# Moving operands of each layer at a byte offset of their own, and a weight ring of four slots, in a four-block encoder

## The chip, the cores and the metric

The kernel runs on one core of a Trainium2 chip. The metric is the device time of one execution in microseconds (us), taken as the median of several runs. The engines are named as in the profile: PE is the matrix engine, PEld its loading of weights, DVE the vector engine, ACT the scalar engine, POOL the general one, and SP issues the DMA transfers.

## What is computed

The reference is a four-block encoder on a sequence of 256 tokens with 1024 features, in float32. Each block has a gated feed-forward layer, a mixer and a second feed-forward layer, so there are twelve layers:

```python
for i in range(DEPTH):                       # DEPTH = 4
    m, j = i % 3, i // 3
    x = x + 0.5 * swiglu(rms_norm(x, norms[i, 0]), ffn_w_in[i, 0], ffn_w_out[i, 0])
    hn = rms_norm(x, norms[i, 1])
    y = short_conv_mixer / hyena_mixer / gated_deltanet_mixer   # m = 0 / 1 / 2
    x = x + y
    x = x + 0.5 * swiglu(rms_norm(x, norms[i, 2]), ffn_w_in[i, 1], ffn_w_out[i, 1])
return rms_norm(x, final_norm)
```

The feed-forward width is 2816, which is 22 tiles of 128. The layers in order are: feed-forward, short convolution, feed-forward, feed-forward, Hyena, feed-forward, feed-forward, gated delta rule, feed-forward, feed-forward, short convolution, feed-forward. The code numbers them by `ng`, 0 to 11.

## The kernel before

Everything that is multiplied by a weight goes through one helper, `mm3`. A float32 number is split into a high part of type fp32r and the remainder, also fp32r, and a product is three matmuls of 128 x 128 weights against 128 x 256 moving columns: high weights with high columns (L324), low weights with high columns (L325), high weights with low columns (L326). The weights are the stationary operand and the tokens the moving one.

**Weights.** All weights are packed on the host into 665 parts of 128 x 1024. `load_group` brings them in two at a time (1 MB, two buffers of two parts). `cut_part` splits a part: ACT writes the high part `wh` (L279), then DVE the low part `wl` (L281). Both go into a ring of RING = 5 slots for each of `wh` and `wl`. One part is used by 24 matmuls. A slot is free again when the last of its 24 matmuls is done.

**Moving operands.** At the end of a layer `split_x` writes the residual stream times the next norm's weight as `xh` (ACT, L344) and `xl` (DVE, L345), four pairs of tiles of 128 x 512, which the next layer's projections read (the tiles `g`, `c`, `b`, `p`, `x`, `xv` in PSUM). Inside a layer `split` writes the activations as `hh` (ACT, L454) and `hl` (DVE, L455), 128 x 256, four slots each, which the output products read (`accf`, `accs`, `acch`, `accd`). A feed-forward layer has 44 projection parts and 22 output parts.

**Layer starts.** `finish` holds the last two parts of a layer at the same time and goes through the four PSUM banks of the output product bank by bank: as soon as a bank is complete, DVE updates `x` (L438, in the Hyena layer L432), and `split_x` and `square_x` follow. The next layer begins with `proj_first`, which takes three parts side by side, so that the last tiles of `x` are wanted late: 6 matmuls of each of the three parts for a first pair of tiles, then again for the second, and so on. The fourth and fifth parts of a layer are held back until the last split of `x` has been issued (`behind`).

**Order of the work.** The program is written in the order of the mathematics; a scheduler of the framework orders the instructions of each engine by its own estimate of when their inputs and buffers are free. Each engine then runs its list strictly in order.

**Places in memory.** From the program's memory map, in bytes within a partition: the ten ring slots begin at 47,360 + 4,096 n, and every 128-column block of weights 512 bytes on, so all weights of the ring begin 256 bytes above a multiple of 512. The tiles `xh` and `xl` also begin 256 above a multiple of 512, `hh` and `hl` 320 above one. For the rest of the text the *distance* of a matmul is the start of its moving operand less the start of its weights, modulo 512. In the kernel before it is 0 for all projections and 64 for the output products. In the Hyena layer the transforms `vf` and `vi`, whose operands are other tiles, have 256, and the last four output parts, whose `hh` and `hl` lie in another pool, have 320.

Of the kernel before, what the change touches and what calls it, by code (L numbers as in the profile page):

```python
# [11 lines left out]
F32 = mybir.dt.float32  # L12
F32R = mybir.dt.float32r
# [5 lines left out]
P = 128  # L19
D = 1024  # L20
L = 256
# [11 lines left out]
RING = 5  # L33
HOLD = 2
VACT = 3
WARM = 16

# [13 lines left out]
# ---------------------------------------------------------------- layouts  # L51
# Weight parts [128, 1024]: ("c", W, c0) = columns c0..c0+127 of W, all 8
# contraction tiles side by side; ("r", W, r0) = rows r0..r0+127 of W.
def out_tiles(f, n):
    """Rows of the output product that follow the projection of tile f."""
    if f <= LAG:
        return []
    lo = 0 if f == LAG + 1 else f - LAG
    return [t for t in range(lo, f - LAG + 1) if t < n - TAIL]
# [120 lines left out]
def shape_tables():  # L180
    f = np.float32
    # masks and ones
# [3 lines left out]
    # positional features of the filter network, transposed  # L186
# [11 lines left out]
    # 512-point transform of 256 samples, frequencies 0..255 and, in place of  # L198
    # the zero sine, the Nyquist one
# [15 lines left out]
# ---------------------------------------------------------------- program  # L215
class Prog:
    def __init__(self, nc, tc, io, phases, pools):
        self.nc, self.tc, self.io, self.phases = nc, tc, io, phases
        self.cp, self.rp, self.tp, self.ps = pools
        self.nparts = len(part_list(phases))  # L220
        self.next_part = 0
        self.raw = {}
# [3 lines left out]
        n = 0  # L226
# [9 lines left out]
    # ---- weight stream  # L236
    def load_group(self, lo, n):
        nc = self.nc
        t = self.rp.tile([P, GRP, D], F32, name=f"raw{lo}", tag="raw", bufs=RAW)
        if lo < 5:  # L240
            # the first parts come in small pieces
# [9 lines left out]
    def load_behind(self, dst, src):  # L251
        """A load that keeps its place behind the weights."""
        with self.tc.issue_after(self.load.ins):
            self.load = self.nc.sync.dma_start(dst, src)
# [31 lines left out]
    def behind(self, i, z):  # L286
        """Parts that a new phase wants late are split behind the split of x."""
# [10 lines left out]
    # ---- products: out[col, tok] (+)= part' @ x  # L298
# [10 lines left out]
    def proj_first(self, outs):  # L309
        """A phase's first products: several parts side by side, so that the  # L310
        last tiles of x are wanted late. outs: (destination, start)."""
# [19 lines left out]
    # ---- residual update, split of x*g, and 1/rms  # L331
# [4 lines left out]
    def split_x(self, m, ng):  # L336
        nc = self.nc
        ph = self.tp.tile([P, 512], F32R, name=f"xh{ng}_{m}", tag=f"xh{m}", bufs=1)
        pl = self.tp.tile([P, 512], F32R, name=f"xl{ng}_{m}", tag=f"xl{m}", bufs=1)
        for k in (2 * m, 2 * m + 1):  # L340
            s = slice((k % 2) * L, (k % 2 + 1) * L)
            xs, xh, xl = self.x[m][:, s], ph[:, s], pl[:, s]
# [18 lines left out]
    def rstd(self, ng, squared=False):  # L361
        """1/rms of the tokens, on every partition. Two stages, each to be
        issued behind other products."""
# [28 lines left out]
    # ---- accumulation of the output product  # L392
# [16 lines left out]
    def finish(self, pend, scale, bias, nxt):  # L409
        """The last output products, bank by bank, each bank's part of the  # L410
        residual stream updated as soon as it is complete."""
# [37 lines left out]
    def split(self, src, name, pool=None):  # L449
        """High and low parts of an SBUF tile."""  # L450
        pool = pool or self.tp
        hh = pool.tile([P, L], F32R, name=f"hh{name}", tag="hh", bufs=4)
        hl = pool.tile([P, L], F32R, name=f"hl{name}", tag="hl", bufs=4)
# [7 lines left out]
    # ---- phases  # L461
# [37 lines left out]
    def conv3(self, out, u, w, j, on_act=True):  # L499
        """out[t] = w0 u[t-1] + w1 u[t] + w2 u[t+1] along the free axis."""  # L500
# [50 lines left out]
    # ---- hyena: filters (spectra of the two-sided filter), then the mixer  # L551
    def sine(self, out, pre, bias, freq, tag):
        """out = sin(freq * (pre + bias)), the argument brought into [-pi, pi]."""
# [16 lines left out]
    def hy_setup(self):  # L570
        """Filter network up to its last layer; the rest goes to the background."""
# [42 lines left out]
        for c in range(2):  # L614
# [3 lines left out]
            def taps(b, c=c, cs=cs, eo=eo):  # L618
# [8 lines left out]
                if b == 0:  # L627
                    nc.vector.memset(hs[1][0:1, :], 0.0)
                    # v * d_bias is the filter's tap at zero
# [34 lines left out]
    def hy(self, ng, nxt):  # L664
# [6 lines left out]
        # constants of the short convolution: b_in enters through its taps  # L671
# [13 lines left out]
        def conv(pt, j, tag, bufs):  # L685
            """short convolution of one bank: columns j[0], j[1] of 128 features"""
# [28 lines left out]
        def turn(pr):  # L715
            """the pair's gated values with tokens on partitions"""
# [98 lines left out]
    # ---- gated delta rule, chunks of 128 tokens, both directions. With A the  # L815
    # strictly triangular matrix of a chunk, columns scaled by
    # gamma = beta / |k|^2, the chunk's solution is w = gamma * (I + A)^-1 r and
    # all products use the unscaled k and q.
    def gd(self, ng, nxt):
# [33 lines left out]
        # a large negative exponent outside the triangles  # L853
# [17 lines left out]
        def gates2(ab):  # L871
# [8 lines left out]
            # log(1 + exp(x)) = max(x, 0) + 2 atanh(u / (2 + u)), u = exp(-|x|)  # L880
# [28 lines left out]
        def decay(rg, hg, b, d):  # L909
            """E[s, c] = exp(sum of g over the tokens after s up to c), 0 outside the triangle"""  # L910
# [8 lines left out]
        def weights():  # L919
            """exp of the sums of g from a token to its chunk's end or start"""  # L920
# [17 lines left out]
        def turn(srcs, name):  # L938
            """[features, tokens] of two heads -> one bank [tokens, block, head, features]"""
# [45 lines left out]
        def kk(pr):  # L985
            """B = transposed -A of both directions"""
# [5 lines left out]
        def later():  # L992
            """Pool's work that nothing waits for yet"""
# [28 lines left out]
        # -- inverses of the 32 x 32 diagonal blocks, one block per partition  # L1022
        inv = {}

        def gather():
# [16 lines left out]
            # M[c, s] and the inverse's transpose X[s, c]; the two 16 x 16 blocks of the diagonal  # L1042
# [11 lines left out]
        def corner(stage, q):  # L1054
            """lower left 16 x 16 block: the second block's inverse times M21 times the first's"""
# [517 lines left out]
```

## Time and profile before

| quantity | value |
|---|---|
| median of 3 runs | 2073.7 us (2072.6 to 2074.67) |
| span of the profiled execution | 2073.3 us |
| PE busy | 2048.9 us, 99% |
| PEld busy | 2028.2 us, 98% |
| DVE busy | 1407.5 us, 68% |
| ACT busy | 1014.2 us, 49% |
| DMA | 356.76 MB, mean 172 GB/s |

The profile counts a matmul from its start to its modelled end, and successive matmuls overlap in it. A matmul that is listed with 283 ns therefore does not take 283 ns of the engine. What one costs is the distance between two starts, which the timeline shows, and which the text calls the pace. The program has few places at which PE stands idle, so that the span is close to the number of matmuls times their pace.

### The profile page before, as it was taken

To read this page: it belongs to the slowest core of one execution; us is meant where nothing else is said; L and a number is where in the kernel's file an instruction comes from. 1 tells how busy PE (TensorE), PEld (TensorE's weight loads), DVE (VectorE), ACT (ScalarE), POOL (GpSimd) and SP (SyncE) were. 2 spreads that over 40 slices of the span, in tenths; PEclk is the share of its full clock that TensorE was granted. 3 is DMA by queue.
4 is the path that set the end of the run, shared out by engine and by line. 5 is a ranking of instruction groups with operands and counts; after the bars stand their busy time and mean duration, and the time that the engine had idled before them with its cause. 6 is when DMAs were issued, how large, how long until landed. Compare 5 with 4: busy or idle time off the path is not lost.

```text
span 2073.3 us, 40294 instructions
## 1 busy us (share of the span) xinstructions
PE 2048.9 (99%) x17234; PEld 2028.2 (98%) x17234; DVE 1407.5 (68%) x2155; ACT 1014.2 (49%) x1546; POOL 73.8 (4%) x75
## 2 busy tenths in 40 slices
PE   9999999999999999999999998999999999999998
PEld 9999999999999999999999998899999999999998
DVE  6766867666666798666766689866667666767664
ACT  6444545445444555444544476555445444545443
POOL 0000000000000110000000021000000000000000
PEclk9999999999999999999999999999999999999999
DMA  7644455555555443555555532315554555555552
GB/s 249 233 164 153 153 183 183 183 183 173 194 183 184 163 158 128 196 184 187 181 184 185 185 123 102 123 62 185 184 184 169 199 185 185 179 185 181 186 186 95
DMA packets 93990, 356.76 MB, mean 172 GB/s; under 512 B 5810, under 2 KB 7218, under 8 KB 93619
## 3 DMA queue, kind: packets, MB, share of 16 engines
q1 hardware_dynamic: 93666, 354.18, 50.1%
q8 instruction: 135, 2.21, 0.4%
q14 instruction: 45, 0.36, 0.1%
q10 hardware_dynamic: 144, 0.00, 0.0%
HBM read 353.11 MB, written 1.05 MB: 171 GB/s over the span
## 4 chain that ended last, share of the span: by engine, by line
PE 89%; DVE 7%; DMA 2%; ACT 1%; issue 1%; POOL 0%; SPq 0%; POOLq 0%; DVEq 0%; ACTq 0%
PE g L324 16%; PE g L326 16%; PE g L325 16%; PE accf L324 8%; PE accf L326 8%; PE accf L325 8%; DVE wl L281 2%; PE c L324 1%; PE c L326 1%; PE c L325 1%; DMA raw<-w 1%; PE b L325 1%; PE b L324 1%; PE b L326 1%; PE accs L324 1%
## 5 line engine op out<-in xcount | busy, mean ns | idle before, releaser
L281 DVE TENSOR_TENSOR wl<-raw,wh 128x1024 fp32r<-128x1024 f32 (+1 forms) x667 | 811.2, 1221 | 430.7 <-ACT wh L279 430.3
L279 ACT ACTIVATE wh<-raw 128x1024 fp32r<-128x1024 f32 (+1 forms) x667 | 696.1, 1051 | 670.4 <-PE g L326 476.5
L324 PE MATMUL g<-xh,wh 128*128 128x256 f32 x2816 | 799.6, 284 | 1.0 <-ACT xh L344 0.7
L326 PE MATMUL g<-xl,wh 128*128 128x256 f32 x2816 | 798.3, 283 | 0.0
L325 PE MATMUL g<-xh,wl 128*128 128x256 f32 x2816 | 797.4, 283 | 0.3 <-DVE wl L281 0.3
L324 PEld LDWEIGHTS g<-xh,wh 128*128 128x128 f32 x2816 | 540.5, 192 | 4.1 <-ACT wh L279 2.8
L325 PEld LDWEIGHTS g<-xh,wl 128*128 128x128 f32 x2816 | 539.9, 192 | 0.6 <-DVE wl L281 0.5
L326 PEld LDWEIGHTS g<-xl,wh 128*128 128x128 f32 x2816 | 539.9, 192 | 0.2 <-DVE xl L345 0.2
L324 PE MATMUL accf<-hh,wh 128*128 128x256 f32 x1408 | 394.8, 280 | 0.0
L326 PE MATMUL accf<-hl,wh 128*128 128x256 f32 x1408 | 393.0, 279 | 0.0
L325 PE MATMUL accf<-hh,wl 128*128 128x256 f32 x1408 | 392.9, 279 | 0.0
L324 PEld LDWEIGHTS accf<-hh,wh 128*128 128x128 f32 x1408 | 264.9, 188 | 1.2 <-ACT hh L454 0.8
L326 PEld LDWEIGHTS accf<-hl,wh 128*128 128x128 f32 x1408 | 264.5, 188 | 0.0
L325 PEld LDWEIGHTS accf<-hh,wl 128*128 128x128 f32 x1408 | 264.2, 188 | 0.1
L454 ACT ACTIVATE hh<-t 128x256 fp32r<-128x256 f32 x192 | 79.8, 416 | 194.0 <-DVE t L474 189.7
L471 DVE TENSOR_TENSOR t<-g,rs 128x256 f32<-128x256 f32 x176 | 74.5, 423 | 83.8 <-PE g L326 77.2
L455 DVE TENSOR_TENSOR hl<-t,hh 128x256 fp32r<-128x256 f32 x192 | 81.4, 424 | 69.8 <-ACT hh L454 69.8
L325 PE MATMUL p<-xh,wl 128*128 128x256 f32 x256 | 74.5, 291 | 8.1 <-DVE wl L281 8.1
L472 ACT ACTIVATE t<-t 128x256 f32<-128x256 f32 x176 | 71.0, 404 | 23.4 <-DVE t L471 23.2
L324 PE MATMUL p<-xh,wh 128*128 128x256 f32 x256 | 75.8, 296 | 1.4 <-ACT wh L279 1.4
L474 DVE TENSOR_TENSOR t<-t,t 128x256 f32<-128x256 f32 x176 | 73.5, 418 | 1.5 <-ACT t L472 1.4
L326 PE MATMUL p<-xl,wh 128*128 128x256 f32 x256 | 74.1, 290 | 0.0
(315 smaller groups left out, 2424.7 us busy)
## 6 DMA issues: line engine op xcount, KB each, us to landing
raw<-w SPq DMA_DIRECT2D x330, 1024.0 KB, 4.8
raw<-w SPq DMA_DIRECT2D x6, 256.0 KB, 5.4
x<-x SPq DMA_DIRECT2D x4, 256.0 KB, 4.8
raw<-w SPq DMA_DIRECT2D x2, 512.0 KB, 6.1
dec<-dec SPq DMA_DIRECT2D x1, 1024.0 KB, 7.0
traw<-dft SPq DMA_DIRECT2D x2, 512.0 KB, 6.2
out<-ob SPq DMA_DIRECT2D x4, 256.0 KB, 2.4
w<-w SPq DMA_DIRECT2D x1, 512.0 KB, 9.0
```

Of the source, the lines that this page charges most:

```text
L279: nc.scalar.activation(hi[:, s], src[:, s], AF.Copy)
L281: nc.vector.tensor_tensor(lo[:, s], src[:, s], hi[:, s].bitcast(F32), op=ALU.subtract)
L324: mm(out, ah, bh, start=start, stop=False, skip_group_check=True)
L325: mm(out, al, bh, start=False, stop=False, skip_group_check=True)
L326: mm(out, ah, bl, start=False, stop=stop, skip_group_check=True)
L454: self.nc.scalar.activation(hh, src, AF.Copy)
L455: self.nc.vector.tensor_tensor(hl, src, hh.bitcast(F32), op=ALU.subtract)
L471: nc.vector.tensor_tensor(t1, pg[f][:, :L], self.rs, op=ALU.mult)
L472: nc.scalar.activation(t1, t1, AF.Silu)
L474: nc.vector.tensor_tensor(t2, t1, t2, op=ALU.mult)
```

## The change

Three things are changed. First, `xh`, `xl`, `hh` and `hl` move into a pool of their own, `mv`, that lies right behind the weights' ring and begins with 256 bytes that nothing uses (`lead`); their slots are 512 bytes longer than the tile (640 columns instead of 512, and 384 instead of 256). Second, the tile begins in its slot at FIRST[ng] columns, a different number in each of the twelve layers. Third, the ring has four slots instead of five, which gives back 8 KB of the 8.25 KB that this needs. In the gated delta rule `xtile` follows its slots into the new pool.

```diff
-RING = 5
+RING = 4
+LEAD = 64
+FIRST = (0, 8, 16, 32, 24, 48, 64, 40, 80, 96, 56, 112, 0)
...
+        self.mv.tile([P, LEAD], F32, name="lead")
...
     def split_x(self, m, ng):
-        ph = self.tp.tile([P, 512], F32R, name=f"xh{ng}_{m}", tag=f"xh{m}", bufs=1)
-        pl = self.tp.tile([P, 512], F32R, name=f"xl{ng}_{m}", tag=f"xl{m}", bufs=1)
+        ph = self.mv.tile([P, 640], F32R, name=f"xh{ng}_{m}", tag=f"xh{m}", bufs=1)
+        pl = self.mv.tile([P, 640], F32R, name=f"xl{ng}_{m}", tag=f"xl{m}", bufs=1)
         for k in (2 * m, 2 * m + 1):
             s = slice((k % 2) * L, (k % 2 + 1) * L)
-            xs, xh, xl = self.x[m][:, s], ph[:, s], pl[:, s]
+            at = slice((k % 2) * L + FIRST[ng], (k % 2 + 1) * L + FIRST[ng])
+            xs, xh, xl = self.x[m][:, s], ph[:, at], pl[:, at]
...
     def split(self, src, name, pool=None):
-        pool = pool or self.tp
-        hh = pool.tile([P, L], F32R, name=f"hh{name}", tag="hh", bufs=4)
-        hl = pool.tile([P, L], F32R, name=f"hl{name}", tag="hl", bufs=4)
+        pool = pool or self.mv
+        at = FIRST[int(name.split("_")[0])]
+        hh = pool.tile([P, 384], F32R, name=f"hh{name}", tag="hh", bufs=4)[:, at:at + L]
+        hl = pool.tile([P, 384], F32R, name=f"hl{name}", tag="hl", bufs=4)[:, at:at + L]
...
         def xtile(tag, name):
-            return self.tp.tile([P, 4, P], F32, name=name, tag=tag, bufs=1)
+            pool = self.tp if tag.startswith("sq") else self.mv
+            return pool.tile([P, 4, P], F32, name=name, tag=tag, bufs=1)
```

In the memory map of the changed program the ring still begins at 47,360, so the weights stay 256 bytes above a multiple of 512, and the slots of `xh`, `xl`, `hh` and `hl` begin at multiples of 512. Projections and output products of one layer now have the same distance, four times FIRST less 256, modulo 512:

| layer `ng` | 0 | 1 | 2 | 3 | 4 | 5 | 6 | 7 | 8 | 9 | 10 | 11 |
|---|---|---|---|---|---|---|---|---|---|---|---|---|
| kind | ff | conv | ff | ff | Hyena | ff | ff | delta | ff | ff | conv | ff |
| offset, bytes | 0 | 32 | 64 | 128 | 96 | 192 | 256 | 160 | 320 | 384 | 224 | 448 |
| distance before, projections | 0 | 0 | 0 | 0 | 0 | 0 | 0 | 0 | 0 | 0 | 0 | 0 |
| distance now | 256 | 288 | 320 | 384 | 352 | 448 | 0 | 416 | 64 | 128 | 480 | 192 |

The number of instructions of each kind stays, and so does the order of SP and POOL. What moves is the place of the weights' splits among the rest on ACT and DVE, since the scheduler has one slot less.

At the start of layer 3 (part 164 is its first, `wh166` and `wl166` belong to the third part of `proj_first`) ACT had this row before:

```order
L454 ACTIVATE hh2_21_5779<-t2_2_21_5774 128x256
L279 ACTIVATE wh166_5923<-raw165_5917 128x1024
L344 ACTIVATE xh3_0_5842<-x0_69,par_67 128x256 x2
L352 ACTIVATE sq3_0_5848<-x0_69 128x512
L344 ACTIVATE xh3_1_5863<-x1_70,par_67 128x256 x2
L352 ACTIVATE sq3_1_5869<-x1_70 128x512
L344 ACTIVATE xh3_2_5885<-x2_71,par_67 128x256 x2
```

Now ACT has this one:

```order
L460 ACTIVATE hh2_21_5783<-t2_2_21_5778 128x256
L283 ACTIVATE wh165_5923<-raw165_5921 128x1024
L349 ACTIVATE xh3_0_5846<-x0_73,par_71 128x256 x2
L357 ACTIVATE sq3_0_5852<-x0_73 128x512
L283 ACTIVATE wh166_5927<-raw165_5921 128x1024
L349 ACTIVATE xh3_1_5867<-x1_74,par_71 128x256 x2
L357 ACTIVATE sq3_1_5873<-x1_74 128x512
L349 ACTIVATE xh3_2_5889<-x2_75,par_71 128x256 x2
```

The third part's high split moved from ahead of the splits of `x` into their middle. On DVE, at the same place, before:

```order
L281 TENSOR_TENSOR wl166_5924<-raw165_5917,wh166_5923 128x1024
L438 SCALAR_TENSOR_TENSOR x0_69<-accf2_0_3987,x0_69 128x512
L345 SCALAR_TENSOR_TENSOR xl3_0_5843<-x0_69,par_67,xh3_0_5842 128x256
L438 SCALAR_TENSOR_TENSOR x1_70<-accf2_1_3988,x1_70 128x512
L345 SCALAR_TENSOR_TENSOR xl3_0_5843<-x0_69,par_67,xh3_0_5842 128x256
L438 SCALAR_TENSOR_TENSOR x2_71<-accf2_2_3989,x2_71 128x512
L345 SCALAR_TENSOR_TENSOR xl3_1_5864<-x1_70,par_67,xh3_1_5863 128x256 x2
L438 SCALAR_TENSOR_TENSOR x3_72<-accf2_3_3990,x3_72 128x512
```

And now:

```order
L285 TENSOR_TENSOR wl165_5924<-raw165_5921,wh165_5923 128x1024
L443 SCALAR_TENSOR_TENSOR x0_73<-accf2_0_3991,x0_73 128x512
L350 SCALAR_TENSOR_TENSOR xl3_0_5847<-x0_73,par_71,xh3_0_5846 128x256
L443 SCALAR_TENSOR_TENSOR x1_74<-accf2_1_3992,x1_74 128x512
L350 SCALAR_TENSOR_TENSOR xl3_0_5847<-x0_73,par_71,xh3_0_5846 128x256
L443 SCALAR_TENSOR_TENSOR x2_75<-accf2_2_3993,x2_75 128x512
L285 TENSOR_TENSOR wl166_5928<-raw165_5921,wh166_5927 128x1024
L350 SCALAR_TENSOR_TENSOR xl3_1_5868<-x1_74,par_71,xh3_1_5867 128x256 x2
L350 SCALAR_TENSOR_TENSOR xl3_2_5890<-x2_75,par_71,xh3_2_5889 128x256 x2
L443 SCALAR_TENSOR_TENSOR x3_76<-accf2_3_3994,x3_76 128x512
```

The third part's low split now stands behind the third update of `x`. It stands so at nine of the eleven layer starts. At the start of layer 5, behind the Hyena layer, DVE now has the third part's split (`wl264`) almost at the end of the splits of `x`, where before it stood ahead of them all:

```order
L437 SCALAR_TENSOR_TENSOR x3_76<-acch4_3_9236,par_71,x3_76 128x256
L350 SCALAR_TENSOR_TENSOR xl5_2_9613<-x2_75,par_71,xh5_2_9612 128x256 x2
L437 SCALAR_TENSOR_TENSOR x3_76<-acch4_3_9236,par_71,x3_76 128x256
L350 SCALAR_TENSOR_TENSOR xl5_3_9627<-x3_76,par_71,xh5_3_9626 128x256
L285 TENSOR_TENSOR wl264_9654<-raw263_9647,wh264_9653 128x1024
L350 SCALAR_TENSOR_TENSOR xl5_3_9627<-x3_76,par_71,xh5_3_9626 128x256
```

The start of layer 1 has the third part's split (`wl68`) in the same way just ahead of the last pair `xl1_3`.

## Rows read from the trace of the kernel before

**Rows 1.** The page, first part, and the chain that ended last.

```profile
PE 2048.9 (99%) x17234; PEld 2028.2 (98%) x17234; DVE 1407.5 (68%) x2155; ACT 1014.2 (49%) x1546; POOL 73.8 (4%) x75
...
PE 89%; DVE 7%; DMA 2%; ACT 1%; issue 1%; POOL 0%; SPq 0%; POOLq 0%; DVEq 0%; ACTq 0%
```

**Rows 2.** Stretch of two feed-forward layers: busy us (count) by engine, clock, DMA.

```profile
core 0: us, PE busy (x) PEld busy (x) DVE busy (x) ACT busy (x) POOL busy (x), PEclk, DMA share, GB/s
840.00:1180.00 340.00, 340.00 (x2852) 340.00 (x2852) 211.37 (x292) 155.24 (x210) 3.01 (x2) 1.00 0.55 185
```

**Rows 3.** The page's groups: busy, mean ns of one | idle before, releaser.

```profile
L281 DVE TENSOR_TENSOR wl<-raw,wh 128x1024 fp32r<-128x1024 f32 (+1 forms) x667 | 811.2, 1221 | 430.7 <-ACT wh L279 430.3
L279 ACT ACTIVATE wh<-raw 128x1024 fp32r<-128x1024 f32 (+1 forms) x667 | 696.1, 1051 | 670.4 <-PE g L326 476.5
```

**Rows 4.** Timeline of PE, start us and us: first and last of four rows.

```profile
539.43 0.28 PE L324 MATMUL accf<-hh,wh 128*128 128x256 f32 x1
...
542.15 0.28 PE L326 MATMUL accf<-hl,wh 128*128 128x256 f32 x1
542.26 0.29 PE L324 MATMUL g<-xh,wh 128*128 128x256 f32 x1
...
547.91 0.28 PE L326 MATMUL g<-xl,wh 128*128 128x256 f32 x1
...
786.22 0.28 PE L324 MATMUL acch<-hh,wh 128*128 128x256 f32 x1
...
788.92 0.28 PE L326 MATMUL acch<-hl,wh 128*128 128x256 f32 x1
...
791.91 0.28 PE L324 MATMUL acch<-hh,wh 128*128 128x256 f32 x1
...
799.96 0.28 PE L326 MATMUL acch<-hl,wh 128*128 128x256 f32 x1
```

**Rows 5.** Tiles `vf` and `sp`: ns min/median/max, first and last start us.

```profile
L325 PE MATMUL vf<-vth,tl x32: 278/283/283, 724.0 to 791.7; 128*128 128x256 f32 x32
...
L325 PE MATMUL sp<-eoh,tl x4: 389/389/389, 250.5 to 252.5; 128*128 128x512 f32 x4
...
L325 PE MATMUL sp<-eoh,tl x2: 393/395/397, 157.1 to 157.8; 128*128 128x512 f32 x2
```

**Rows 6.** Timeline at the start of layer 3: ACT, DVE, PE.

```profile
499.11 1.04 ACT L279 ACTIVATE wh<-raw 128x1024 fp32r<-128x1024 f32 x1
...
502.86 0.62 ACT L352 ACTIVATE sq<-x 128x512 f32<-128x512 f32 x1
...
503.99 0.68 DVE L438 SCALAR_TENSOR_TENSOR x<-accf,x 128x512 f32<-128x512 f32 x1
...
509.87 2.35 DVE L281 TENSOR_TENSOR wl<-raw,wh 128x1024 fp32r<-128x1024 f32 x2
...
504.33 0.29 PE L324 MATMUL g<-xh,wh 128*128 128x256 f32 x1
...
513.34 0.36 PE L324 MATMUL g<-xh,wh 128*128 128x256 f32 x1
```

**Rows 7.** Timeline at the start of layer 5: DVE, PE.

```profile
815.01 0.47 DVE L345 SCALAR_TENSOR_TENSOR xl<-x,par,xh 128x256 fp32r<-128x256 f32 x1
...
812.55 0.28 PE L324 MATMUL g<-xh,wh 128*128 128x256 f32 x1
```

**Rows 8.** Tile `wl` from 1200 to 1330 us, delta-rule layer: who waited for it.

```profile
  PEld p L325: 8.5, 2
```

More of the change, by code (lines that the diff above doesn't have):

```diff
@@ L218, in __init__ @@
         self.nc, self.tc, self.io, self.phases = nc, tc, io, phases
-        self.cp, self.rp, self.tp, self.ps = pools
+        self.cp, self.rp, self.mv, self.tp, self.ps = pools
         self.nparts = len(part_list(phases))
         self.next_part = 0
+        self.mv.tile([P, LEAD], F32, name="lead")
         self.raw = {}
@@ L1545, in build @@
         with tc.tile_pool(name="cp", bufs=1) as cp, tc.tile_pool(name="rp", bufs=1) as rp, \
-                tc.tile_pool(name="tp", bufs=1) as tp, \
+                tc.tile_pool(name="mv", bufs=1) as mv, tc.tile_pool(name="tp", bufs=1) as tp, \
                 tc.tile_pool(name="ps", bufs=1, space=bass.MemoryType.PSUM) as ps:
-            Prog(nc, tc, io, phases, (cp, rp, tp, ps)).run()
+            Prog(nc, tc, io, phases, (cp, rp, mv, tp, ps)).run()
 def arrays(inp, phases):
```

## The prediction
> **What bounds the kernel now.** The page and the chain first [rows 1]: PE is busy 99% of 2073.3 us, and 89% of the chain is PE. Then a stretch without a layer of another kind [rows 2]: 2852 matmuls in 340.00 us, 119.2 ns each, at full granted clock (2.4 GHz), with no idle time. So in the feed-forward layers the time is the number of matmuls times their pace, and only a change of the pace or a new hole in PE's row can be seen. The count does not change.
>
> The pace is not one number. From first and last starts in the timeline [rows 4]: a run of 48 projections `g` takes 547.91 - 542.26 = 5.65 us for 47 steps, 120.2 ns; a run of 24 output products `accf` 2.72 us for 23, 118.3 ns; in the Hyena layer one run of `acch` 2.70 us for 23, 117.4 ns, and the next 72 only 8.05 us for 71, 113.4 ns. All are 256 columns of fp32r on full weights at full clock. Between the projections' pace and the best run lie 6.8 ns, and there are some 11,000 projections, so this is where the change can act. ACT waits for PE to free a slot for 476.5 us in all and DVE waits for ACT for 430.3 us [rows 3]: the splits run as far ahead as the ring lets them.
>
> **The moved operands.** What differs between these runs? Projections have distance 0, `accf` and the 117.4 run 64; of the 113.4 run the first 48 have 64 and the last 24 have 320 (`hh` of the other pool). `vf`, at distance 256, has the listed duration of a matmul at 120, 283 ns [rows 5]. I read this as two streams that PE reads at once, the columns of one matmul and the weights of the next, which hold each other up by an amount that the distance sets: 0 and 256 the worst, 64 and 320 better. Against it: at distance 64 both 118 and 113.4 occur, and `sp` (512 columns, distance 0) is listed with 389 ns in one place and 395 in another [rows 5], so that the distance doesn't fix the pace alone; and all slow runs change their moving tile from one triple to the next while the `acc` runs keep theirs, so the kind of loop could be the cause.
>
> Counted by layer, with 24 matmuls a part: a feed-forward layer has 1056 projections at 120 and 528 output products at 118, 1584 at a mean of 119.3. Layers 0 and 6 get distance 256 and 0: their output products go from 118 to 120, 528 x 2 ns = 1.1 us each, +2.1 together. Layer 2 gets 320, 113.4: 1584 x -5.9 = -9.3. Layer 8 gets 64, which is mostly 118: 1584 x -1.3 = -2.1. Layers 3, 5, 9 and 11 get 384, 448, 128 and 192, at which no run stands. Their bounds are the fastest and the slowest rows, 113.4 and 120; I take the middle, 116.7, since nothing places them nearer to either: 1584 x -2.6 = -4.1 each, -16.5 together (ends -9.3 and +1.1 each). The other layers get odd multiples of 32 and are taken at 116.7 too: convolution, 768 matmuls at a mean of 119.5, -2.2 twice; Hyena, 768 at 118.6, -1.5; delta rule, 984 at 119.6, -2.9; together -8.7 (ends -19.5 and +2.3). Sum **-34.5 us**, ends -73 and +11.
>
> The Trainium skill speaks against this: "SBUF — State Buffer" says under "SBUF: two separate sides" that TensorE's port never waits for anyone, and "TensorE: Matmul & The Clock Gate" under "Step-by-step: what each phase is for" gives TensorE two independent read ports, one for the moving operand and one for weights. By these the two streams cannot meet, no distance matters, and the sum would be 0 instead of -34.5, the first rival below. The trace's three paces for equal matmuls [rows 4] sit badly with it, but no run here changes an address alone.
>
> ACT's and DVE's writes of `xh`, `xl`, `hh`, `hl` have the same count and shape. I cost their new offsets at nothing: both engines wait for PE for hundreds of us, which hides some ns each.
>
> **The ring of four.** In steady state a part is split when a slot comes free, and takes 1.05 + 1.22 us [rows 3]; a part lasts 24 x 0.119 = 2.86 us. With five slots it is ready 4 x 2.86 - 2.3 = 9.1 us ahead, with four 6.3. The loads follow the splits, so they shift along. Cost 0, as long as a load is not 6 us late.
>
> At a layer start the cover is gone. The last two parts are held to the end, so with four slots only two of the three parts of `proj_first` fit before. At the start of layer 3 the third part was split from 499.11 on [rows 6]; now it needs the slot of the last part but one, and stands on ACT behind the first square (502.86 + 0.62), then on DVE behind the third update of `x`. That update ends at 503.99 + 0.68 = 504.67, so `wl` is there at 504.67 + 1.22 = 505.9. PE wants it as the 14th matmul of the layer: 504.33 + 13 x 0.12 = 505.9. Just in time. Behind it the splits of `x` come 1.2 us later, and PE has 2.2 us for each pair; the fourth part's `wl` came at 509.87 + 1.2 = 511.1 and is wanted at 513.34 + 0.2, which leaves about 1 us after the shift. I take 0.2 us for each of nine starts, 1.8 (ends 0 and 1.2 each).
>
> Two starts are worse. At layer 5 DVE now has the split behind the seventh `xl`, which ended at 815.01 + 0.47 = 815.5; plus 1.22 that is 816.7, and PE wants it at 812.55 + 0.12 [rows 7]: **4 us** of waiting. Layer 1 has the split just as late in the list and gets the same, so 8 for both (ends 3 and 9).
>
> In the Hyena and delta-rule layers DVE is the engine that ends last for stretches; waits for `wl` there cost PE 8.5 us [rows 8]. One part less is split before such a stretch: 1.2 us each, 2.4 (ends 0 and 2.9 each). Ring in all **+12 us**, ends 3 and 25.
>
> **Sum** against the profiled execution: 2073.3 - 34.5 + 12 = 2050.8 us. Its span is 0.4 below the median of the runs, so 2051.
>
> **Rivals.** *The address does nothing* (pace by the kind of loop, or by something that follows the order of the matmuls). For it: the mixture at distance 64, and the pages named. Then only the ring is left: 2073.7 + 12 = 2086, slower. It decides if projections stay at 120 in layers 2, 3, 8 and 9. Chance 0.24.
> *All new distances are as good as the best run.* For it: the worst distances are the ones where both starts agree modulo 256, and eight layers leave them. Then six feed-forward layers give -9.3 each, the others -19.5, with +2.1 and +12: 2013. Chance 0.16.
> *Only distances that the trace shows as better help*, the rest stay at their mean: +2.1 - 9.3 - 2.1 + 12, 2076. Chance 0.12.
> *The new distances are as bad as the worst*: +11 + 12, 2097. Chance 0.06.
> *The scheduler's list hurts more than I think*, each start waiting 1.2 us and both late ones 4.5, with the forecast's gain: 2073.7 - 34.5 + 25 = 2064, still faster; it is within the forecast.
>
> **How the numbers follow.** The forecast has 0.42, from 2032 (half of the unknown to the floor, ring 3 us cheaper) to 2069. With 0.2% (4.1 us), about what a measurement of this kernel can tell from no change, as the bound, faster is 0.42 + 0.16 = 0.58. Of the third rival 0.08 is within the bound and 0.04 beyond, of the first 0.02 within: same 0.10. Slower is 0.22 + 0.04 + 0.06 = 0.32. The range reaches from the second rival's 2013, a little below, to just above the first's 2086: 2010 to 2088 leaves out the fourth rival and some of the second.
>
> **What would show it.** In the timeline of the changed kernel `g` and `accf` of one layer have one pace, and it differs between layers: 120 in layers 0 and 6, about 113 in layer 2. If `g` stays at 120 in every layer, the first rival holds. At the start of layer 5 PE should stand idle for about 4 us some 1.4 us after its first `g`, waiting for `wl`, and the same at layer 1; at the other starts less than 0.3. If the feed-forward stretches show new holes, the ring is worth more than 12. The forecast is wrong if paces above 121 appear, or if the pace changes within a layer.

## The result and the profile after

The changed kernel takes **2048.19 us** in the median (2045.12 to 2064.86), the kernel before 2074.18 beside it: a ratio of 0.9888, with a 95% interval of 0.9856 to 0.992. So it is faster, by 1.1% or 23 us by the ratio (17 to 30). The profiled execution took 2051.18 us, of which the span is 2049.3.

The same two rows as [rows 1], from the page of after (busy time by engine; shares of the chain that ended last):

```profile
PE 2019.6 (99%) x17234; PEld 1995.7 (97%) x17234; DVE 1415.9 (69%) x2155; ACT 1014.9 (50%) x1546; POOL 75.2 (4%) x75
...
PE 90%; DVE 6%; ACT 2%; issue 1%; DMA 0%; POOL 0%; POOLq 0%; DVEq 0%; ACTq 0%
```

PE is still busy 99% of the span, with the same 17234 matmuls, and its busy time is 29.3 us shorter (2048.9 - 2019.6); the span is 24.0 us shorter. The matmuls got faster, and some 5 us of waits came in between.

Where did they get faster? The view of [rows 2], of after, 140 us from the middle of each feed-forward layer (layers 0, 2, 3, 5, 6, 8, 9, 11 in this order: stretch, busy us and number of instructions of PE, of PEld, DVE, ACT and POOL, granted clock, DMA share, GB/s):

```profile
45.00:185.00 140.00, 140.00 (x1109) 135.07 (x1108) 92.39 (x136) 64.27 (x88) 0.00 (x0) 1.00 0.55 191
343.00:483.00 140.00, 140.00 (x1238) 140.00 (x1237) 88.53 (x120) 65.32 (x86) 0.00 (x0) 1.00 0.57 196
530.00:670.00 140.00, 140.00 (x1182) 140.00 (x1181) 85.52 (x116) 62.08 (x82) 0.00 (x0) 1.00 0.53 183
830.00:970.00 140.00, 140.00 (x1238) 140.00 (x1237) 88.17 (x119) 65.63 (x86) 0.00 (x0) 1.00 0.56 195
1015.00:1155.00 140.00, 140.00 (x1169) 140.00 (x1169) 83.18 (x113) 61.77 (x81) 0.00 (x0) 1.00 0.53 182
1412.00:1552.00 140.00, 140.00 (x1238) 140.00 (x1237) 89.24 (x120) 65.14 (x86) 0.00 (x0) 1.00 0.57 196
1595.00:1735.00 140.00, 140.00 (x1182) 140.00 (x1182) 84.94 (x115) 61.77 (x81) 0.00 (x0) 1.00 0.54 188
1880.00:2020.00 140.00, 140.00 (x1191) 140.00 (x1190) 85.48 (x116) 63.04 (x83) 0.00 (x0) 1.00 0.55 188
```

PE never stops and the clock is 1.00 (2.4 GHz) in all of them, so the count is the pace. Layer 0 can't be compared (in it other matmuls run in between, some of 512 columns, as `sp` [rows 5]). The others fall into four groups: 1238 matmuls, about 113 ns each (layers 2, 5 and 8, distances 320, 448 and 64); 1191, 117.5 ns (layer 11, distance 192); 1182, 118.4 ns (layers 3 and 9, distances 384 and 128); 1169, 119.8 ns (layer 6, distance 0). The edges of a stretch cost such a count a matmul or two; the gaps between successive starts give 113.3, 117.8, 118.7 and 120.0 ns, and these figures are used from here on. Before, every one of these layers made a mixture of 120 and 118 [rows 2, 4].

The splits are as they were [rows 3], from the page of after: the same counts and means, with less idle time on DVE since PE asks for them sooner.

```profile
L285 DVE TENSOR_TENSOR wl<-raw,wh 128x1024 fp32r<-128x1024 f32 (+1 forms) x667 | 812.5, 1221 | 410.4 <-ACT wh L283 409.6
L283 ACT ACTIVATE wh<-raw 128x1024 fp32r<-128x1024 f32 (+1 forms) x667 | 698.4, 1052 | 638.9 <-PE g L330 471.7
```

### The profile page after: what moved, and what is told of

It is laid out like the page before. It is cut to its first block, busy times and chain, and to the rows that moved or that the text cites. A ratio compares the mean times of both kernels' runs of the same rounds, so it can differ in the third digit from the quotient of the medians.

```text
span 2049.3 us, 40302 instructions
## 1 busy us (share of the span) xinstructions
PE 2019.6 (99%) x17234; PEld 1995.7 (97%) x17234; DVE 1415.9 (69%) x2155; ACT 1014.9 (50%) x1546; POOL 75.2 (4%) x75
## 4 chain that ended last, share of the span: by engine, by line
PE 90%; DVE 6%; ACT 2%; issue 1%; DMA 0%; POOL 0%; POOLq 0%; DVEq 0%; ACTq 0%
PE g L330 16%; PE g L328 16%; PE g L329 16%; PE accf L330 7%; PE accf L328 7%; PE accf L329 7%; DVE wl L285 2%; PE c L330 1%; DVE xl L350 1%; PE c L328 1%; PE c L329 1%; ACT wh L283 1%; PE p L329 1%; PE p L330 1%; PE p L328 1%
## 5 line engine op out<-in xcount | busy, mean ns | idle before, releaser
L330 PE MATMUL g<-xl,wh 128*128 128x256 f32 x2816 | 789.4, 280 | 2.2 <-DVE xl L350 2.2
L329 PE MATMUL g<-xh,wl 128*128 128x256 f32 x2816 | 789.5, 280 | 1.4 <-DVE wl L285 1.1
L328 PE MATMUL g<-xh,wh 128*128 128x256 f32 x2816 | 790.7, 281 | 0.1
L328 PEld LDWEIGHTS g<-xh,wh 128*128 128x128 f32 x2816 | 534.2, 190 | 3.1 <-ACT wh L283 2.6
L330 PEld LDWEIGHTS g<-xl,wh 128*128 128x128 f32 x2816 | 532.6, 189 | 3.4 <-DVE xl L350 3.4
L329 PEld LDWEIGHTS g<-xh,wl 128*128 128x128 f32 x2816 | 533.0, 189 | 2.6 <-DVE wl L285 2.5
```

The source lines that it names most:

```text
L328: mm(out, ah, bh, start=start, stop=False, skip_group_check=True)
L329: mm(out, al, bh, start=False, stop=False, skip_group_check=True)
L330: mm(out, ah, bl, start=False, stop=stop, skip_group_check=True)
```

## The experiments

The theory: the pace of a matmul is set by the distance between the start of the columns that PE reads and the start of the weights that it loads (modulo 512, as in the table of the change), and by nothing else of the address. Rivals: the address does nothing; the absolute place of the moving operand counts; the new slots or their place count, not the offsets. Beside this, the ring's cost was to be measured alone.

### The ring alone (e1_ring4)

```diff
-RING = 5
+RING = 4
```

> The kernel before with a ring of four slots and nothing else: the starts of the moving operands and of the weights keep their distances (0 for projections, 64 for output products). If the pace is set by that distance, projections stay at 120 ns and output products at 118 in every layer, and the whole difference is the ring: by the prediction +12 us (3 to 25), 2086, with PE idle for about 4 us each near the starts of layers 1 and 5. By the changed kernel's trace, where each layer start cost PE only about 1 us more than before, it is rather +5 to +10, 2079 to 2084.

Measured: 2081.9 us (2081.27 to 2083.18) against 2073.6, ratio 1.004 (1.0025 to 1.0055): **+8.3 us** (5 to 11), under the prediction's +12 and inside the range that was taken from the changed kernel's trace. What PE waited for, in the view of the waits (who waited <- for whom: us in all, times, longest); first the largest of the kernel before, which is the 8.1 behind [rows 8], then five of the ring of four alone:

```profile
PE p L325 <- DVE wl L281: 8.1, 2, 5.0
PE accd L324 <- ACT hh L454: 2.2, 1, 2.2
...
PE p L324 <- ACT wh L279: 1.4, 1, 1.4
```

```profile
PE p L325 <- DVE wl L281: 10.2, 4, 6.4
PE p L324 <- ACT wh L279: 2.7, 1, 2.7
...
PE g L326 <- DVE xl L345: 2.0, 6, 0.4
...
PE g L325 <- DVE wl L281: 1.3, 2, 0.9
...
PE c L326 <- DVE xl L345: 0.7, 2, 0.4
```

Two things have grown. In the delta-rule layer `p` waits 10.2 + 2.7 instead of 8.1 + 1.4 us, 3.4 more. And at the layer starts there is a wait that this view did not list before, of `g` and `c` for `xl`, never over 0.4 us: the third part's split now stands between the splits of `x`, which come later for it. In the changed kernel the same view gives nearly the same numbers:

```profile
PE p L329 <- DVE wl L285: 10.4, 4, 6.4
PE p L328 <- ACT wh L283: 2.7, 1, 2.7
...
PE g L330 <- DVE xl L350: 2.2, 6, 0.4
...
PE g L329 <- DVE wl L285: 1.1, 3, 0.8
```

### The weights moved, the columns left in place (e3_weights)

```diff
         self.cp, self.rp, self.tp, self.ps = pools
+        self.rp.tile([P, 16], F32, name="pad")
+        self.tp.tile([P, 112], F32, name="pad2")
```

The first block puts 64 bytes ahead of the ring. The second puts 448 bytes ahead of the rest, which so moves on by 512 in all and keeps its place modulo 512.

> The kernel before with the weights' ring moved by 64 bytes and every other operand where it was. The moving operands keep their places; only their distance from the weights changes, from 0 to 448 for projections and from 64 to 0 for output products. If the distance between the two streams is what counts, projections get faster (113.4 to 118 ns, as layers 5 and 11 of the changed kernel) and output products slower (120), about 2011 to 2060 in all. If the absolute place of the moving operand is what counts, nothing changes: 120 and 118 ns, 2074.

Measured: 2028.35 us (2026.97 to 2029.4), ratio 0.978 (0.9766 to 0.9795), with five slots and without any new offset. The groups of the page, mean ns of one after the comma:

```profile
L326 PE MATMUL g<-xh,wh 128*128 128x256 f32 x2816 | 784.0, 278 | 0.4 <-ACT wh L281 0.3
...
L328 PE MATMUL accf<-hl,wh 128*128 128x256 f32 x1408 | 398.3, 283 | 0.0
```

Before it was the other way round, 284 for `g` and 280 for `accf`. And the timeline of PE in layer 3, a run of 24 output products and one of 48 projections, first and last start, as in [rows 4]:

```profile
525.72 0.28 PE L326 MATMUL accf<-hh,wh 128*128 128x256 f32 x1
...
528.46 0.28 PE L328 MATMUL accf<-hl,wh 128*128 128x256 f32 x1
528.58 0.29 PE L326 MATMUL g<-xh,wh 128*128 128x256 f32 x1
...
533.93 0.28 PE L328 MATMUL g<-xl,wh 128*128 128x256 f32 x1
```

The output products make 2.74 us for 23 steps, 119.1 ns (118.3 before), the projections 5.35 us for 47, 113.8 ns (120.2 before). The moving operands kept their places modulo 512, and PE's matmuls their order (but for four short ones of the delta rule); the weights moved by 64 bytes and the two kinds of products changed roles. So the kind of loop, the order and the place of the columns alone are out. The place of the weights alone is out by the changed kernel, where they keep theirs and the paces differ from layer to layer. The distance is left. In the prediction the first rival had the support of the Trainium skill: "TensorE: Matmul & The Clock Gate", under "Step-by-step: what each phase is for", says that loading the next weights doesn't take read bandwidth from the running matmul. This run does not agree: 64 bytes between the two cost or give 6 ns of 120.

### All offsets set to one value (e4_all256)

```diff
-FIRST = (0, 8, 16, 32, 24, 48, 64, 40, 80, 96, 56, 112, 0)
+FIRST = (0,) * 13
```

> The changed kernel with all its offsets set to the first one: the longer slots, their place and the ring of four stay, the distance is 256 in every layer. If the distance sets the pace, projections and output products run at 120 ns in all layers, as in layer 0 of the changed kernel, some 6000 output products lose 2 ns each (+12), and with the ring's 5 to 12 us the time is 2090 to 2098, slower than before. If the gain came from the new places or the longer slots rather than from the offsets, it stays at about 2050.

Measured: 2090.8 us (2090.49 to 2091.18), ratio 1.0082 (1.0067 to 1.0097). With everything of the change but the offsets, the kernel is slower than before, and two feed-forward layers (2 and 3) show the count of layer 6 of after:

```profile
345.00:485.00 140.00, 140.00 (x1169) 140.00 (x1168) 83.74 (x113) 60.89 (x81) 0.00 (x0) 1.00 0.53 181
537.00:677.00 140.00, 140.00 (x1169) 140.00 (x1169) 83.35 (x113) 61.64 (x81) 0.00 (x0) 1.00 0.53 182
```

The longer slots and their new place bring no gain; the offsets are worth 42.6 us between this kernel and the changed one.

### One good distance everywhere (e2_all64, e5_all320, e6_all448)

Five slots again, the slots of `xh`, `xl`, `hh` and `hl` at their old length, and one distance for all twelve layers, set by the block ahead of them. Against the changed kernel, for 64 (320 and 448 have LEAD = 80 and 112):

```diff
-RING = 4
+RING = 5
-LEAD = 64
+LEAD = 16
-FIRST = (0, 8, 16, 32, 24, 48, 64, 40, 80, 96, 56, 112, 0)
+FIRST = (0,) * 13
...
-        ph = self.mv.tile([P, 640], F32R, name=f"xh{ng}_{m}", tag=f"xh{m}", bufs=1)
+        ph = self.mv.tile([P, 512], F32R, name=f"xh{ng}_{m}", tag=f"xh{m}", bufs=1)
...
-        hh = pool.tile([P, 384], F32R, name=f"hh{name}", tag="hh", bufs=4)[:, at:at + L]
+        hh = pool.tile([P, 256], F32R, name=f"hh{name}", tag="hh", bufs=4)[:, at:at + L]
```

> Five slots as before, and all moving operands of the twelve layers at one distance, 64 bytes from the weights' start modulo 512. If the distance sets the pace, every layer leaves 120 ns: at the best run's 113.4 everywhere the time is about 1979, at the 118 of the output products of before about 2052; which of the two it takes tells whether distance 64 alone is enough for the best run. If the distance were idle and the gain of the changed kernel came from elsewhere, 2074.

> As the kernel with distance 64 everywhere, but 320, which is 64 modulo 256. If the effect repeats every 256 bytes, each layer of it runs at 113.3 or at 117.8 ns as there, layer by layer, and the time lies between 1979 and 2052, near that kernel's 2017. If 320 is a better distance than 64 (layer 2 of the changed kernel and the last 24 matmuls of the Hyena layer before ran at 113.3 at 320), all layers run at 113.3 and the time is about 1980. If the repeat is 512 and 320 is like any other, something else.

> Distance 448, which is 192 modulo 256, everywhere, five slots. With the moved weights the projections at 448 ran at 113.8 to 115 ns in every layer, with output products at 120 between them; layer 5 of the changed kernel ran at 113.3 throughout. If 448 always falls into the fast state, about 1980 to 1990. If the fast state there came from the output products at 120 between them, which set the engine's phase anew each time, layers differ here as they do at distance 64, between 1990 and 2045.

Measured: 64 gives 2017.32 us (2012.56 to 2026.69), ratio 0.9743 (0.9719 to 0.9767); 320 gives 2019.75, ratio 0.9738 (0.9723 to 0.9752); 448 gives 2016.04, ratio 0.9724 (0.9701 to 0.9746). All three beat the changed kernel by about 30 us, some 8 of which are the fifth slot by e1_ring4. None reaches 1980. The stretches say why; layers 2 and 3 at distance 64, and the same two at 320:

```profile
340.00:480.00 140.00, 140.00 (x1191) 140.00 (x1190) 85.42 (x115) 61.97 (x82) 0.00 (x0) 1.00 0.54 187
525.00:665.00 140.00, 140.00 (x1237) 140.00 (x1237) 88.22 (x119) 65.58 (x86) 0.00 (x0) 1.00 0.56 195
```

```profile
340.00:480.00 140.00, 140.00 (x1191) 140.00 (x1190) 85.01 (x114) 62.53 (x82) 0.00 (x0) 1.00 0.54 185
525.00:665.00 140.00, 140.00 (x1238) 140.00 (x1237) 88.93 (x120) 64.48 (x85) 0.00 (x0) 1.00 0.57 196
```

In the long stretches of layers 1 to 10 the two kernels agree in which layer is quick; that is what a repeat of 256 bytes asks for. And one distance has two paces: 1238 matmuls in 140 us in one layer, 1191 in the next, 113.3 or 117.8 ns, and nothing between in these stretches. Layer 2 is slow here at 320, the distance at which it is quick in the changed kernel. At 448 the long stretches of layers 2, 5, 9 and 11 have the first and those of layers 1, 3, 6, 8 and 10 the second. The prediction had met this in the mixture at distance 64 [rows 4] and could not place it.

What chooses? At 448, the timeline of PE at the start of layer 3, where the pace changes (matmuls left out at "..."):

```profile
487.65 0.28 PE L328 MATMUL g<-xh,wh 128*128 128x256 f32 x1
...
495.70 0.28 PE L330 MATMUL g<-xl,wh 128*128 128x256 f32 x1
495.81 0.50 PE L375 MATMUL pst<-msk,sq 128*128 128x1 f32 x4
...
496.61 0.28 PE L328 MATMUL g<-xh,wh 128*128 128x256 f32 x1
...
498.96 0.28 PE L330 MATMUL g<-xl,wh 128*128 128x256 f32 x1
```

The 72 matmuls ahead of the four short `pst` (the sums of squares for the norm) take 495.70 - 487.65 = 8.05 us for 71 steps, 113.4 ns; behind them it is 498.96 - 496.61 = 2.35 us for 20 steps, 117.5. From there the layer keeps that pace to its end: in the gaps of successive starts it changes only where something else comes in between, at `pst`, at `pbc` (the 1/rms), at a wait, or at a step from one distance to another. A layer that came to its `pst` at 113.3 to 113.6 left it at 117.6 or 117.7, in all 24 cases from layer 2 on in the three kernels with 448 (this one and two below). It looks like a phase between the two streams, which an interruption can set anew and which is kept as long as matmuls of the same kind follow each other; this is a reading of the paces, and no run looks into the streams themselves.

### Setting the pace on purpose (e8_kick448, e9_kick64, e10_kick1)

In the long stretches of e3_weights each step from an output product at distance 0 to a projection at 448 had been followed by 113.3. So every fourth output part (24 matmuls, which share one `hh` and `hl`) gets a pair of slots of its own, which lies at distance 0, ahead of the block that shifts the rest:

```diff
+        self.mv.tile([P, L], F32R, name="h0", tag="h0", bufs=1)
+        self.mv.tile([P, L], F32R, name="l0", tag="l0", bufs=1)
         self.mv.tile([P, LEAD], F32, name="lead")
...
+        th, tl, n = "hh", "hl", 4
+        if pool is self.mv:
+            th, tl, n = ("h0", "l0", 1) if int(name.split("_")[1]) % 4 == 0 else ("hh", "hl", 3)
+        hh = pool.tile([P, L], F32R, name=f"hh{name}", tag=th, bufs=n)
+        hl = pool.tile([P, L], F32R, name=f"hl{name}", tag=tl, bufs=n)
```

The second kernel has the same with 64 in place of 448. In the third the pair is somewhat longer, and only the first output part of a layer lies at 0:

```diff
+        zero = name.split("_")[1] == "0"
+        wh, ah = (368, 0 if zero else 112) if n == 1 else (L, 0)
+        wl, al = (272, 16 if zero else 0) if n == 1 else (L, 0)
```

> As the kernel with 448 everywhere, but every fourth output product reads a pair of slots at distance 0. In the kernel with the moved weights each step from an output product at 0 to a projection at 448 was followed by 113.3 ns within six matmuls. If such a step always leads into the fast state, the layers that ran at 117.8 (3, 6 and 8, and the short 1 and 10) run at 113.3 from their first output products on: 0.88 x 7.1 us for each long one and half of it for a short one, -25, against +7.5 for a quarter of the output products at 120: 2016 - 25 + 7.5 = 1999. If the state is drawn anew at each step, the layers get a mixture and the time is about 2020 to 2025.

> The same with distance 64 in place of 448. In the kernel before, every step from a projection at 0 to an output product at 64 in the feed-forward layers was followed by 118 ns. If the distances on both sides of the step fix the state, all feed-forward layers run at 117.8 from their first output products on, also those (3, 6, 8, 9, 11) that ran at 113.3 with 64 alone: 2017 + 5 x 6.3 + 3 + 7.5 = about 2055 to 2060. If any step from 0 leads into the fast state, about 2000 as at 448.

> As the kernel with 448 and a fourth of the output products at 0, but only the first output product of each layer at 0. If the state, once reached, lasts until the next layer's sums of squares, one step per layer is enough: the same paces and 4 to 6 us less for the output products that are not at 0 any more, about 1994. If it does not last, between this and 2016.

Measured: 2006.21 us (2005.39 to 2007.48), ratio 0.9675 (0.9661 to 0.9689), for the first; 2050.86, one run, for the second; **2000.66** (1999.32 to 2001.36), ratio 0.9646 (0.963 to 0.9662), for the third. Layer 3 of the third, which had 117.8 at 448 without the step: projections ahead of the step, the output part at 0, projections behind it (the output part between them, at 448, is left out), and the stretch that follows.

```profile
500.00 0.28 PE L332 MATMUL g<-xl,wh 128*128 128x256 f32 x1
...
510.95 0.28 PE L332 MATMUL g<-xl,wh 128*128 128x256 f32 x1
511.07 0.28 PE L330 MATMUL accf<-hh,wh 128*128 128x256 f32 x1
...
513.83 0.28 PE L332 MATMUL accf<-hl,wh 128*128 128x256 f32 x1
...
516.69 0.28 PE L330 MATMUL g<-xh,wh 128*128 128x256 f32 x1
...
522.01 0.28 PE L332 MATMUL g<-xl,wh 128*128 128x256 f32 x1
```

```profile
517.00:657.00 140.00, 140.00 (x1238) 140.00 (x1237) 88.25 (x119) 65.59 (x86) 0.00 (x0) 1.00 0.57 196
```

Ahead of the step it is 10.95 us for 93 steps, 117.7 ns; at 0, 2.76 us for 23, 120.0; behind it 5.32 us for 47, 113.2.

Layers 3 and 6 at distance 64 with the step, both of which had 1237 without it:

```profile
527.00:667.00 140.00, 140.00 (x1189) 140.00 (x1188) 85.04 (x114) 62.26 (x82) 0.00 (x0) 1.00 0.54 184
1010.00:1150.00 140.00, 140.00 (x1188) 140.00 (x1187) 85.29 (x115) 62.94 (x82) 0.00 (x0) 1.00 0.54 188
```

Behind one step 0 to 448 all seven feed-forward layers from layer 2 on run at 113.3 to their end. Five of them (3, 5, 6, 9 and 11) had 117.8 up to the step, as had the convolution of layer 10, which changes in the same way; layers 2 and 8 had come to 113.3 ahead of it. The convolution of layer 1 ran at 113.3 behind the step for 24 matmuls and was back at 117.8 after the next interruption.

Behind every step 0 to 64 these seven layers run at 117.8, but all seven had that pace when the first step came, so that they show only that the step does not lead into the quick pace. That it can end it is seen in layer 0 of that kernel, where twice a stretch at 113.3 became 117.9 behind an output part at 0. So the pace can be set, and in the long stretches it lasts to the end of the layer.

The first and the third kernel missed their expectations by about 7 us. By the lengths of the layers, third against e6_all448, the three slow long layers (3, 6 and 8) got 6.0 to 6.2 us shorter, as expected (0.88 x 7.1). But layers 1 and 10 got 0.1 and 2.0 shorter in place of 3.1 each; layers 5, 9 and 11 got 0.4 to 0.6 longer, since a layer that comes in at 113.3 now runs at 117.8 from its `pst` to its first output part, about 8 to 23 us behind its start; and the Hyena and the delta-rule layer got 0.8 and 1.4 longer. The second kernel came out 4 to 9 us under its expectation, for one thing because at 64 a step to 120 costs 2.2 ns from 117.8, not the 6.7 that I had put for all. The third kernel beats both kernels of this study: it is 48 us under the changed one.

### Twelve more distances (e7_sweep)

```diff
-FIRST = (0, 8, 16, 32, 24, 48, 64, 40, 80, 96, 56, 112, 0)
+FIRST = (4, 60, 12, 20, 28, 44, 52, 36, 14, 18, 10, 46, 0)
```

> The changed kernel with another table of offsets, so that one profile shows the pace at twelve more distances modulo 256: 16, 240, 48, 80, 112, 176, 208, 144, 56, 72, 40, 184 in layers 0 to 11. If the pace depends on the distance in steps of 64 bytes or 32, each of these has the pace of a neighbour already seen (120 at 0, 116.7 at 32, 113.3 or 117.8 at 64, 119.8 at 96, 118.6 at 128, 118.4 at 160, 113.3 or 117.7 at 192, 118.3 at 224). If it is smooth, values between. A distance that gives less than 113.3, or 113.3 in both kinds of products with no second state beside it, is the one to use. Time between 2030 and 2085.

Measured: 2069.71 us, one run. Layers 2, 5, 6, 8 and 9, distances 48, 176, 208, 56 and 72 modulo 256:

```profile
340.00:480.00 140.00, 140.00 (x1185) 140.00 (x1185) 84.81 (x114) 62.12 (x82) 0.00 (x0) 1.00 0.54 188
...
833.00:973.00 140.00, 140.00 (x1176) 140.00 (x1175) 84.36 (x113) 61.52 (x82) 0.00 (x0) 1.00 0.54 187
1023.00:1163.00 140.00, 140.00 (x1202) 140.00 (x1201) 86.18 (x116) 62.98 (x83) 0.00 (x0) 1.00 0.55 189
1418.00:1558.00 140.00, 140.00 (x1169) 140.00 (x1168) 84.37 (x113) 60.82 (x80) 0.00 (x0) 1.00 0.54 185
1610.00:1750.00 140.00, 140.00 (x1169) 140.00 (x1168) 83.58 (x113) 61.44 (x81) 0.00 (x0) 1.00 0.53 183
```

Neither steps nor a smooth curve. 56 and 72 lie 8 bytes to either side of the best distance and run at 120 in these stretches, as do 40 and 184: all four that are no multiple of 16. The multiples of 16 lie between 116.7 and 119.3 in the long layers (48 and 80 at 118.3, 176 at 119.3, 208 at 116.7); 112 came to 114.3 in the Hyena layer's projections. No distance was better than 113.3. More than one pace at one distance is not a matter of 64 and 192 alone: 208 went from 119.1 to 116.7 and 80 from 120.0 to 118.3 within the first 13 us of a layer, 72 from 118.3 to 120.0, and 16, in the often interrupted layer 0, had stretches at 116.7, 118.7 and 113.5.

### The changed kernel a second time (e11_again)

> The changed kernel once more, with nothing changed, for a second profile of it; its times so far lie between 2045 and 2065. If the spread comes from the two states at odd multiples of 64, the layers at other distances have the paces of the first profile to 0.3 ns, and only layers 2, 5, 8 and 11 (113.3, 113.3, 113.3 and 117.7 ns there) may have changed, each for about 7 us: 2044 with all four fast, 2051 with one slow, 2058 with two, 2065 with three. If it comes from elsewhere, all layers are a little longer or shorter.

Measured: 2049.78 us, one run. Layers 5 and 11 in this profile:

```profile
833.00:973.00 140.00, 140.00 (x1191) 140.00 (x1191) 85.19 (x114) 62.37 (x82) 0.00 (x0) 1.00 0.54 188
...
1882.00:2022.00 140.00, 140.00 (x1237) 140.00 (x1237) 88.56 (x121) 65.32 (x86) 0.00 (x0) 1.00 0.55 194
```

In the first profile it was 1238 and 1191: the two layers have changed roles, one 6.5 us longer and the other 6.4 shorter, and the other ten keep their mean paces to within 0.4 ns. (Within the delta-rule layer, at distance 416, single stretches differ: one of 71 projections ran at 120.0 ns in the first profile and at 118.7 in the second.) So at these distances the pace of a layer differs from one execution to the next, and the spread of the kernel's times, 2045 to 2065, has the size of a few such layers. That the other runs differ by this and by nothing else was not looked at.

## Why the prediction came out right

2051 was predicted and 2048.19 measured, with the mechanism that it named: the distance sets the pace. That it came so close is in part luck, as the terms show. The ring's kernel allows a comparison term by term, since after minus e1_ring4 is the offsets, with the slots' length and place, which brought no gain in e4_all256. Lengths of the layers in us, from the first projection of one to the first of the next (the last one to the end of the span):

| layer | distance | before | ring alone | after | offsets: measured | offsets: predicted |
|---|---|---|---|---|---|---|
| 0 | 256 | 209.8 | 209.0 | 210.4 | +1.4 | +1.1 |
| 1 convolution | 288 | 99.2 | 100.5 | 98.5 | -2.0 | -2.2 |
| 2 | 320 | 189.9 | 190.2 | 181.3 | -9.0 | -9.3 |
| 3 | 384 | 189.7 | 190.4 | 189.7 | -0.7 | -4.1 |
| 4 Hyena | 352 | 117.1 | 117.0 | 118.0 | +1.0 | -1.5 |
| 5 | 448 | 190.1 | 190.9 | 181.6 | -9.3 | -4.1 |
| 6 | 0 | 189.7 | 190.4 | 191.7 | +1.4 | +1.1 |
| 7 delta rule | 416 | 206.9 | 207.6 | 207.9 | +0.3 | -2.9 |
| 8 | 64 | 189.7 | 190.2 | 181.2 | -9.0 | -2.1 |
| 9 | 128 | 189.7 | 190.4 | 189.7 | -0.7 | -4.1 |
| 10 convolution | 480 | 92.4 | 93.1 | 92.2 | -0.9 | -2.2 |
| 11 | 192 | 203.8 | 204.3 | 201.8 | -2.5 | -4.1 |

The offsets made -30.6 us in the span (2049.3 - 2079.9; the start of layer 0 is the rest), against -34.5; the ring +6.6 in the span and +8.3 in the medians, against +12. Each sum is too large by some 4 or 5 us, and the two errors cancel. Nor are the measured terms fixed: layers 5 and 11 change by some 6.5 us between the two profiles of this kernel, layers 2 and 8 stand at distances with two paces as well, and the kernel's four times lie between 2045 and 2065.

**The step from pace to distance** held: layers with the known distances 0, 256 and 320 came within 0.4 us of their terms, `g` and `accf` of one layer have one pace in the long stretches, and the weights' shift showed that it is the distance. Layer 2 is luck all the same: at 320 it ran at 113.3 in both profiles of the changed kernel, but at 117.8 in e5_all320, where it took 187.7 us in place of the 189.9 of before, a term of -2.2. And one of the prediction's own signs of being wrong did appear: in layers 2 and 8 the pace changes within the layer, from 117.8 to 113.3 behind `pbc`, 12.7 us after the start, and in layer 5 behind `pst`. A pace that the distance alone sets could not do that.

**The middle for the unknown distances** was right for none of the four layers: it gave -4.1 each, and they made -0.7, -9.3, -0.7 and -2.5. Their sum, -13.2, is near the -16.5 because the ends that I took from the trace, 113.4 and 120, were true ends, and because one of layers 5 and 11 was quick and the other slow, in either profile; with both slow it would have been about -7, with both quick about -20. A middle of two known ends was a fair value for the sum of four unknowns, not for any one.

**Layer 8** was mis-sized, -2.1 for -9.0. I took distance 64 at 118, which the mixture in [rows 4] suggested; the mixture was two paces of one distance, and behind this layer's `pbc` it was the other one. No row of before could tell which.

**The mixers** at odd multiples of 32 gave -1.6 in place of -8.7: 288 came as taken, at 116.7, but 352 is as slow as 0, 480 is at 118.3, and 416 has stretches between 117.3 and 120.0.

**The ring at layers 1 and 5** was to cost 4 us each and cost 1.2 and 0.8. The arrival of `wl` was worked out well: 5.6 us behind the first `g` of layer 5, and it took 5.2. The step that failed is "PE wants it at 812.55 + 0.12" [rows 7]: that is the order of before. PE's row at this place in the changed kernel (start, us, and in brackets what it waited for):

```profile
807.26 0.28 PE L329 MATMUL g<-xh,wl 128*128 128x256 f32 x1
808.32 0.38 PE L329 MATMUL g<-xh,wl 128*128 128x256 f32 x1 [0.78 <-DVE wl L285]
```

The first `g` starts at 803.14; the last matmul ahead of the wait starts 4.1 us after it, not 1.4, and the wait is 0.8 us long. The trace has 36 matmuls ahead of it, where the prediction counted 13: the scheduler has put the other two parts' products with the second and third pair of `x` ahead of the third part's. An order that a scheduler makes has to be read from the changed kernel, where the wait is priced, too.

**The other starts** cost 0.3 to 0.7 us instead of 0.2: mostly the waits for `xl` of up to 0.4 us in the list above, which I had taken as covered, since `xl` comes 1.2 us later and PE has 2.2 us for each pair. **The delta-rule layer** waited 3.4 us longer for weights, with 2.4 predicted for it and the Hyena layer together; 0.7 of it is left in the layer's length.

## What to carry to other kernels

Equal matmuls at full clock can differ by 6% in pace, and a PE that is busy 99% of the time does not show it: count matmuls per stretch, or take successive starts. If the counts differ between loops, compare the start addresses of the moving operand and the weights; moving one of them by 64 bytes costs a small pad and gave 2% here, more than the change with its longer slots and its smaller ring. One distance that is known to be good, used everywhere, is worth more than a table of different ones, and a ring slot given up for room is paid at each start of a layer.

## What the runs showed of the hardware that was not expected

The pace of 256 columns of fp32r on full weights depends on the distance between the two starts, and distances that are 256 bytes apart have the same paces (64 and 320, 0 and 256, 128 and 384). In the long stretches it was 120.0 ns at 0 and at the four distances tried that are no multiple of 16, either 113.3 or 117.8 at 64 and 192, and 116.7 to 119.9 at most others. Eight bytes beside the best distance cost 6.7 ns against its quicker pace.

At 64 and 192 the pace is a matter of history: a few short matmuls in between can change it, it then holds for more than a thousand matmuls, and at 192 (layers 5 and 11 of the changed kernel) it was seen to differ between two executions of one program, 113.3 in one and 117.8 in the other. Other distances (16, 80, 160 and 208 modulo 256) have more than one pace too, in shorter stretches. A step from distance 0 to 448 was followed by 113.3 in all feed-forward layers that were looked at, one from 0 to 64 by 117.8. What in the memory repeats after 256 bytes, and why the one pace lasts as long as the other, stays open.
